# Three pieces of the mixers' elementwise work change engine: two to ScalarE, one to GpSimd

## The chip, the cores and the metric

The kernel runs on one core of a Trainium2 chip. The metric is the device time of one execution in microseconds. The core's engines are TensorE (PE: matmuls and, overlapping with them, weight loads, PEld), VectorE (DVE), ScalarE (ACT), GpSimd (POOL) and SyncE (SP, which here issues most of the DMAs). Each engine runs its own list of instructions in order; an instruction that waits holds up all that stand behind it on the same engine.

## What is computed (the reference, cut)

One decoder layer on 1024 tokens and 16 meta tokens, float32, model width 1024: half-step SwiGLU, then two mixers on the same normalised input, merged by gates, then another SwiGLU and a norm. The mixers are what matters here: a chunked gated DeltaNet (8 heads of 128) and an RWKV-7 time mixing (16 heads of 64).

```python
u = _rmsnorm(h, mix_norm[l])
aq, ak, av, az, abeta, aalpha, bcols, ga, gb = jnp.split(u @ w_in[l], ...)
o_a = _deltanet_branch(...)      # A
o_b = _rwkv7_branch(...)         # B
merged = sigmoid(ga) * o_a + sigmoid(gb) * o_b
h = h + merged @ w_out[l]

# A, per head and chunk of tokens
tinv = triangular_solve(m + eye, eye, lower=True, unit_diagonal=True)
k_tail = k * jnp.exp(g_last[..., None] - g)[..., None]
v_new = u_i - w_i @ state
o = qg_i @ state + attn_i @ v_new
state = state * exp(gl_i) + kt_i.T @ v_new

# B, the decay
w_log = -softplus(-(w0 + jnp.tanh(wd) @ w_up)) - 0.5
decay = exp(-exp(w_log))
a = sigmoid(a0 + ad @ a_up)
```

`k_tail`, the inverses and the two up-projections `w_up` and `a_up` are the three places that the change touches.

## The kernel before

The kernel has three stages: the first feed-forward block, the mixers (`middle`, about 700 to 2290 us of the profile) and the second feed-forward block. Tensors lie with channels on the 128 partitions and tokens along the free dimension. Every dense product is made of three float32r products: an operand is split into a high part (rounded, by ScalarE, L163) and a low part (the rest, by VectorE's subtraction, L164), and `mm3` (L315) multiplies high by high, high by low and low by high; the result is called `pp`, the split weights `w`, the raw ones `wraw`.

The mixers work on two segments of tokens: segment 0 has the 16 meta tokens and 512 others (528 columns, taken as 256 and 272), segment 1 has 512. For each segment there are eight iterations, one for a pair of B's heads and one of A's, so 16 in all. An iteration is made of actions that a table (`schedule`, L171) interleaves, so that three iterations are under way at once: `merge_blocks` and `transitions` of one, `operands` and `inverses` of the next, `chains`, `gates` and `finish` of the first again, then `decay`, `new_b` and `new_a` of the one after the next. From the program in this order a static scheduler makes each engine's list, by its own estimates of when operands are ready. So one edit can move instructions on all engines; nothing is reordered at run time.

The actions that matter:

- `decay` loads the raw up-projections (`upr`), makes their high parts `upz` on ScalarE (L1361) and the low parts by two 64x128 subtractions on VectorE (L1363). The products `pw` and `pa` (L1368 to L1373) use them.
- `new_b` makes B's `vB`, `kB`, `rB`, the normalised key `kkn`, the operands `AR` and `BK`, and at its end `bv` (L1438). ScalarE splits `bv` (`hl`, L163) and TensorE sums its columns (`bon`, L1289, one product with the high part and one with the low part).
- `new_a` makes A's `kq` after a short convolution (`acc`, L1466, with the carry `xr` from GpSimd) and transposes `Va` (L1478, L1479).
- `operands` (L1600 and on) transposes A's keys in four 128x128 pieces into PSUM (`ktp`), and multiplies them by `kts`, one number per partition and piece, into `ktl`. `chains` uses `ktl` one iteration later in `p3` (L1830), the update of the state. `ktl` has two buffers.
- `inverses` solves the triangular systems of all blocks by substitution on VectorE (`tb`, `Xb`, L1657 and L1659, 31 steps of two instructions), then makes a transposed copy `Yt` of the solution `Xb` (L1660). Both go by way of DRAM into `Xc` and `Y`.
- `merge_blocks` joins the blocks on TensorE (`iv`, L1692; `T` is its copy, L1713), and `transitions` uses the result (`xp`, `vp` with the copies `xa`, `at`, `xv`, L1753 to L1759).
- `chains` runs four chunks one after the other. Each has `p` (L1815), a difference on VectorE (`rhA`), `p` (L1821), a copy with a scale on ScalarE (`vn`, L1825), then `pq` (L1827, L1828) and `p` (L1830).
- `gates` makes `zg`, `gs` and `gg` by three activations each (L1211 to L1213).

Of the kernel before, what the change touches and what calls it, by code (L numbers as in the profile page):

```python
# [29 lines left out]
NCA = FULL // CA  # L30
# [1020 lines left out]
def middle(g):  # L1051
    tc, nc = g.tc, g.nc
    g.mmctx.close()
    with ExitStack() as ctx:
# [70 lines left out]
def tmp_tile(g, name, w=528):  # L1125
    return g.st.tile([P, w], F32, name=name, tag="tmp", bufs=NTMP)


def ch3(ap, c):
    return ap.rearrange("p (a b) -> p a b", b=c)  # L1130
# [151 lines left out]
def halves(n, first=256):  # L1282
    return [(0, first), (first, n - first)] if n > 512 else [(0, n)]
# [63 lines left out]
def decay(g, it):  # L1347

    nc, st, V = g.nc, g.st, g.V
    c = g.seg  # L1350
    q = K()
    q.c, q.it, q.j, q.s, q.n, q.off = c, it, it % NJ, c.s, c.n, c.off
    j, n, off = q.j, c.n, c.off
    meta = q.s == 0
    fs = slice(off, off + FULL)
    tmp = lambda name, w=528: tmp_tile(g, name, w)

    raw = st.tile([P, 2, P], F32, name="upr", tag="upr")
    nc.sync.dma_start(raw, g.a["upwa"][j])
    up = g.upz  # L1360
    nc.scalar.activation(up[:, 0:2, :], raw, AF.Copy)  # L1361
    for i, sl in enumerate(HS):
        nc.vector.tensor_tensor(up[sl, 2 + i, :], raw[sl, i, :], up[sl, i, :].bitcast(F32), op=ALU.subtract)  # L1363
    Ls, sw, av = tmp("Ls"), tmp("sw"), tmp("av")
    for c0, cn in halves(n):
        pw = g.mx.tile([P, 512], F32, name="pw", tag="mx")
        cs = slice(c0, c0 + cn)
        nc.tensor.matmul(pw[:, :cn], lhsT=up[:, 0, :], rhs=c.ws[:, cs], start=True, stop=False)  # L1368
        nc.tensor.matmul(pw[:, :cn], lhsT=up[:, 2, :], rhs=c.ws[:, cs], start=False, stop=True)
        nc.scalar.activation(sw[:, c0 : c0 + cn], pw[:, :cn], AF.Exp, scale=-1.0, bias=V("w0", j))  # L1370
        pa = g.mx.tile([P, 512], F32, name="pa", tag="mx")
        nc.tensor.matmul(pa[:, :cn], lhsT=up[:, 1, :], rhs=c.as_[:, cs], start=True, stop=False)
        nc.tensor.matmul(pa[:, :cn], lhsT=up[:, 3, :], rhs=c.as_[:, cs], start=False, stop=True)  # L1373
        nc.scalar.activation(av[:, c0 : c0 + cn], pa[:, :cn], AF.Exp, scale=-1.0, bias=V("a0", j))
    for x in (sw, av):
        nc.scalar.activation(x[:, :n], x[:, :n], AF.Ln, bias=1.0)
        nc.scalar.activation(x[:, :n], x[:, :n], AF.Exp, scale=-1.0)
    nc.vector.tensor_tensor_scan(Ls[:, :n], g.C("rsB")[:, 16 - off : 16 - off + n], sw[:, :n], 0.0,
                                 op0=ALU.mult, op1=ALU.add)
    EN = sw  # L1380
    nc.scalar.activation(EN[:, :n], Ls[:, :n], AF.Exp, scale=CDEC)
    ELx = tmp("ELx", 520).rearrange("p (c t) -> p c t", t=CB + 1)
    nc.gpsimd.memset(ELx[:, :, 0:1], 1.0)
    nc.scalar.activation(ELx[:, :, 1:], ch3(Ls[:, fs], CB), AF.Exp, scale=-CDEC)
    gam = q.gam = st.tile([P, NCB], F32, name="gam", tag="gam", bufs=2)
    nc.gpsimd.tensor_copy(gam.unsqueeze(2), ELx[:, :, CB : CB + 1])
    if meta:
        elm = q.elm = st.tile([P, 17], F32, name="elm", tag="elm", bufs=2)
        nc.gpsimd.memset(elm[:, 0:1], 1.0)
        nc.scalar.activation(elm[:, 1:17], Ls[:, 0:16], AF.Exp, scale=-CDEC)  # L1390
    q.EN, q.ELx, q.av = EN, ELx, av
    return q
# [94 lines left out]
def operands(g, q):  # L1487

    nc, st, V, c, j, n, off = g.nc, g.st, g.V, q.c, q.j, q.n, q.off
# [9 lines left out]
    for c4 in range(0, NCB, 4):  # L1499
        ps = [g.mx.tile([P, 512], F32, name="grb", tag="mx") for _ in range(2)]  # L1500
# [8 lines left out]
    if meta:  # L1509
        nc.vector.tensor_copy(g.bkpm[0:64, 0, :], g.bkm[0:64, :])  # L1510
        nc.vector.tensor_copy(g.bkpm[64:128, 1, :], g.bkm[64:128, :])
        ps = g.mx.tile([P, 512], F32, name="gbm", tag="mx")
        for h in range(2):
# [3 lines left out]
                                op=ALU.mult)  # L1517
# [3 lines left out]
    kts = st.tile([P, NCA], F32, name="kts", tag="kts")  # L1521
# [16 lines left out]
    for b in range(2):  # L1538
        ps = g.mx.tile([P, 512], F32, name="gra", tag="mx")
        for c2 in range(2):  # L1540
            i = 2 * b + c2
# [28 lines left out]
    ps = [g.mx.tile([P, 512], F32, name="bkt", tag="mx") for _ in range(2)]  # L1570
# [21 lines left out]
    if meta:  # L1592
        btm = q.btm = st.tile([64, P], F32, name="btm", tag="btm", bufs=2)
        ps = g.mx.tile([P, 512], F32, name="btp", tag="mx")
        nc.tensor.matmul(ps[:64, 0:P], lhsT=g.bkm, rhs=g.C("ident"), start=True, stop=True)
        nc.scalar.activation(btm, ps[:64, 0:P], AF.Copy)
    ktl = q.ktl = st.tile([P, NCA, P], F32, name="ktl", tag="ktl", bufs=2)
    ps = g.mx.tile([P, 512], F32, name="ktp", tag="mx")
    for i in range(NCA):
        nc.tensor.transpose(ps[:, i * P : (i + 1) * P], kq[:, 0, off + i * CA : off + (i + 1) * CA], g.C("ident"))  # L1600
    nc.vector.tensor_tensor(ktl, ch3(ps, P), kts.unsqueeze(2).to_broadcast([P, NCA, P]), op=ALU.mult)
    if meta:
        vkm = q.vkm
        ps = g.mx.tile([P, 512], F32, name="vmp", tag="mx")
# [33 lines left out]
def inverses(g, q):  # L1638

    nc, st = g.nc, g.st  # L1640
    meta = q.s == 0
    U = g.Ub
    npt = 115
    nblk = NBLK + 3 * meta
    scX = g.dram.tile([NBLK, 32, 2, 16], F32, name="scX", tag="scX", bufs=2)
    scY = g.dram.tile([NBLK + 3, 16, 2, 32], F32, name="scY", tag="scY", bufs=2)
    X = st.tile([115, 32, 16], F32, name="Xb", tag="Xb")
    Yt = st.tile([115, 16, 32], F32, name="Yt", tag="Yt")
    tmb = st.tile([115, 144], F32, name="tb", tag="tb")
    nc.gpsimd.memset(X, 0.0)  # L1650
    Xf = X.rearrange("p t c -> p (t c)")
    nc.gpsimd.memset(Xf[0:64, 0 : 33 * 15 + 1 : 33], 1.0)
    nc.gpsimd.memset(Xf[64:115, 16 : 16 + 33 * 15 + 1 : 33], 1.0)
    for i in range(31):
        nt, ncc = 31 - i, i // 2 + 1
        tv = tmb[:, : nt * ncc].rearrange("p (t c) -> p t c", c=ncc)
        nc.vector.tensor_tensor(tv, U[:, i, i + 1 :].unsqueeze(2).to_broadcast([npt, nt, ncc]),  # L1657
                                X[:, i, 0:ncc].unsqueeze(1).to_broadcast([npt, nt, ncc]), op=ALU.mult)
        nc.vector.tensor_tensor(X[:, i + 1 :, 0:ncc], X[:, i + 1 :, 0:ncc], tv, op=ALU.add)  # L1659
    nc.vector.tensor_copy(Yt, X.rearrange("p t c -> p c t"))  # L1660
    for r in range(2):
        nc.sync.dma_start(scX[:, :, r, :], X[64 * r : 64 * r + NBLK])
    for r in range(2):
        nc.sync.dma_start(scY[:nblk, :, r, :], Yt[64 * r : 64 * r + nblk])
    Y, XA = g.Y[q.it % 2], g.XA
    Xc = q.Xc = st.tile([P, 12, 2, 16], F32, name="Xc", tag="Xb")
    nc.sync.dma_start(Xc.rearrange("p t r c -> p t (r c)"), scX.rearrange("(t b) i r c -> (b i) t (r c)", b=4))
    yv = scY[:NBLK].rearrange("(t b) c r i -> b (c r) t i", b=4)
    for b in (1, 3, 0, 2):
        sl = slice(32 * b, 32 * b + 32)  # L1670
        nc.sync.dma_start(Y[sl, :, 32 * b : 32 * b + 32], yv[b])
        if b < 2:
            nc.gpsimd.tensor_copy(XA[sl, :, b, :, :], Xc[sl, NCB:])
    if meta:
        ym = q.ym = st.tile([48, 3, 16], F32, name="ym", tag="ym", bufs=2)
        ymv = scY[NBLK:, 0:8].rearrange("t c r i -> (c r) t i")
        nc.sync.dma_start(ym[32:48, 0:2], ymv[:, 0:2, 0:16])
        nc.sync.dma_start(ym[0:16, 2], ymv[:, 2, 0:16])
# [205 lines left out]
def finish(g, q):  # L1884
# [110 lines left out]
```

## Time and profile before

| | |
|---|---|
| median of 3 runs | 2974.12 us (2969.96 to 2985.99) |
| the profiled execution | 2974.08 us |
| its span, first to last instruction | 2972.3 us |
| mean granted TensorE clock | 0.993 |

How to read the views: "busy" is the time in which an engine had an instruction running. A row of the timeline has the start in us from the span's start, the duration, engine, line, operation, out<-in, the shape of the output and the input, a count of merged neighbours and, in square brackets, how long the engine was idle before it and what ended that. A row of the waits has the waiting line, what released it, the sum in us, how often, and the longest. Durations on one engine overlap a little, so the distance from one start to the next is shorter than the duration. A tile's row has the shortest, median and longest duration in ns and the first and last start.

### The profile page before, as it was taken

How to read it: one execution, taken by the hardware profiler on the slowest of the kernel's cores; microseconds unless marked ns; L12 is line 12 of the kernel's file. 1: busy time of each engine (PE TensorE's matmuls, PEld its weight loads, DVE VectorE, ACT ScalarE, POOL GpSimd, SP SyncE). 2: the span in 40 equal slices, each digit the busy share in tenths (PEclk: the TensorE clock that was granted, in tenths of full speed). 3: DMA queues.
4: the chain of work that ended last, by engine and by line, in shares of the span. 5: the costliest groups of instructions: out<-in, count | busy, mean ns of one | idle time of the engine just before them, and what ended most of it. 6: DMA issues, size and time to landing. Idle time of an engine off the chain costs nothing.

```text
span 2972.3 us, 63124 instructions
## 1 busy us (share of the span) xinstructions
PE 2876.8 (97%) x25720; PEld 2496.4 (84%) x25720; DVE 2208.8 (74%) x4121; ACT 1450.5 (49%) x2559; POOL 503.4 (17%) x578
## 2 busy tenths in 40 slices
PE   8999999999899999999998999999999999999998
PEld 8999999999878888888776777777777888888887
DVE  8666668776667877788878887778876766667886
ACT  6322234346555656565566556556644422223443
POOL 0332232323000000000000000001101032332431
PEclk9999999999999999999999999999999999999999
DMA  5333236553232322333232332333345332333763
GB/s 212 125 108 108 98 124 206 182 193 118 71 70 72 86 65 68 84 81 85 89 98 73 80 79 77 76 87 82 106 132 185 127 109 99 97 102 130 248 220 113
DMA packets 287907, 339.39 MB, mean 114 GB/s; under 512 B 172704, under 2 KB 181024, under 8 KB 287616
## 3 DMA queue, kind: packets, MB, share of 16 engines
q1 hardware_dynamic: 283600, 326.17, 36.0%
q0 software_dynamic: 2000, 6.56, 0.6%
q8 instruction: 202, 3.31, 0.5%
q10 hardware_dynamic: 2016, 2.63, 0.2%
q14 instruction: 89, 0.73, 0.1%
HBM read 267.63 MB, written 73.41 MB: 115 GB/s over the span
## 4 chain that ended last, share of the span: by engine, by line
PE 67%; DVE 19%; ACT 6%; issue 3%; DMA 3%; SPq 1%; POOL 0%; DVEq 0%; ACTq 0%; POOLq 0%
PE pg L521 25%; PE pp L315 15%; PE pd L742 10%; DVE w L164 3%; PE pwo L315 2%; PE pg L545 2%; DVE tb L1657 1%; DVE Xb L1659 1%; DVE form L164 1%; ACT w L163 1%; PE vp L1342 1%; DMA form<-frm 1%; PE mp L1342 1%; PE xp L1342 1%; PE np L1342 1%
## 5 line engine op out<-in xcount | busy, mean ns | idle before, releaser
L315 PE MATMUL pp<-uk,w 128*128 128x512 f32 (+2 forms) x4824 | 971.3, 347 | 13.8 <-DVE w L164 5.9
L315 PEld LDWEIGHTS pp<-uk,w 128*128 128x128 f32 x4824 | 745.4, 191 | 111.7 <-DVE w L164 14.7
L742 PE MATMUL pd<-form,w 128*128 128x256 f32 (+2 forms) x2904 | 437.3, 312 | 5.4 <-DVE w L164 5.2
L742 PEld LDWEIGHTS pd<-form,w 128*128 128x128 f32 x2904 | 402.7, 189 | 39.5 <-DVE w L164 7.3
L521 PE MATMUL pg<-bt,w 128*128 128x256 f32 (+2 forms) x2520 | 401.9, 318 | 3.1 <-DVE w L164 2.5
L521 PEld LDWEIGHTS pg<-bt,w 128*128 128x128 f32 x2520 | 360.2, 188 | 37.3 <-DVE w L164 3.8
L527 DVE TENSOR_TENSOR c<-c,pg 128x520 f32<-128x520 f32 (+1 forms) x280 | 189.4, 688 | 239.1 <-PE pg L521 215.8
L164 DVE TENSOR_TENSOR w<-wraw,w 128x1024 fp32r<-128x1024 f32 (+1 forms) x254 | 338.2, 1332 | 38.7 <-ACT w L163 37.1
L521 PE MATMUL pg<-b,w 128*128 128x256 f32 (+2 forms) x2160 | 348.1, 317 | 0.0
L163 ACT ACTIVATE w<-wraw 128x1024 fp32r<-128x1024 f32 (+1 forms) x254 | 266.9, 1052 | 164.1 <-PE pg L521 117.4
L521 PEld LDWEIGHTS pg<-b,w 128*128 128x128 f32 x2160 | 309.9, 188 | 28.3 <-DVE w L164 0.3
L163 ACT ACTIVATE w<-wrx 128x1024 fp32r<-128x1024 f32 (+1 forms) x64 | 58.4, 912 | 279.0 <-PE pg L521 239.2
L491 POOL TENSOR_TENSOR wrx<-wrx 128x512 f32<-128x512 f32 x38 | 52.5, 1381 | 612.8 <-DVE w22b L164 351.6
L164 DVE TENSOR_TENSOR form<-form 128x520 fp32r<-128x520 f32 (+1 forms) x152 | 145.8, 995 | 14.0 <-ACT form L163 13.8
L163 ACT ACTIVATE w<-wsum 128x768 fp32r<-128x768 f32 x96 | 75.6, 788 | 155.8 <-PE pd L742 117.1
L164 DVE TENSOR_TENSOR w<-wsum,w 128x768 fp32r<-128x768 f32 x96 | 112.9, 1181 | 37.3 <-ACT w L163 37.3
L163 ACT ACTIVATE form<-form 128x520 fp32r<-128x520 f32 (+1 forms) x152 | 93.8, 631 | 79.5 <-DMA form<-frm 73.4
L242 POOL TENSOR_TENSOR wsum<-wsum,wraw 128x768 f32<-128x768 f32 (+1 forms) x48 | 97.6, 2050 | 204.7 <-DMA wraw<-in_wdn 154.3
L1659 DVE TENSOR_TENSOR Xb<-Xb,tb 115x126 f32<-115x126 f32 (+22 forms) x496 | 125.2, 252 | 8.7
L1657 DVE TENSOR_TENSOR tb<-Ub,Xb 115x126 f32<-115x126 f32 (+22 forms) x496 | 124.5, 251 | 9.5 <-DMA Ub<-scr 2.0
L1466 DVE SCALAR_TENSOR_TENSOR acc<-xr,pk,acc 128x528 f32<-128x528 f32 (+1 forms) x144 | 109.0, 757 | 20.6 <-ACT acc L1462 19.9
L315 PE MATMUL pwo<-uk,w 128*128 128x512 f32 x384 | 95.3, 397 | 1.3 <-DVE uk L164 0.6
(439 smaller groups left out, 4421.4 us busy)
## 6 DMA issues: line engine op xcount, KB each, us to landing
wraw<-in_win SPq DMA_DIRECT2D x150, 512.0 KB
wraw<-in_wgu SPq DMA_DIRECT2D x44, 512.0 KB
wrx<-in_wgu SPq DMA_DIRECT2D x44, 512.0 KB
frm<-c SPq DMA_DIRECT2D x76, 260.0 KB
form<-frm SPq DMA_DIRECT2D x76, 260.0 KB
frm<-c SPq DMA_DIRECT2D x76, 256.0 KB
form<-frm SPq DMA_DIRECT2D x76, 256.0 KB
wraw<-in_wdn SPq DMA_DIRECT2D x34, 384.0 KB
```

Of the source, the lines that this page charges most:

```text
L163: g.nc.scalar.activation(hi, src, AF.Copy)
L164: (eng or g.nc.vector).tensor_tensor(lo, src, hi.bitcast(F32), op=ALU.subtract)
L242: g.nc.gpsimd.tensor_tensor(s, x, y, op=ALU.add if r == 1 else ALU.subtract)
L315: g.last_product = g.nc.tensor.matmul(ps, lhsT=l, rhs=r, start=i == 0, stop=i == n - 1)
L521: nc.tensor.matmul(ps[:, c0 : c0 + cn], lhsT=l[:, x, k, :], rhs=r[:, k, y, c0 : c0 + cn], start=i == 0, stop=i == 3 * HK - 1)
L527: nc.vector.tensor_tensor(o, x, y, op=ALU.add)
L545: nc.tensor.matmul(ps[:, c0 : c0 + cn], lhsT=l[:, x, k, :], rhs=r[:, k, y, c0 : c0 + cn], start=i == 0, stop=i == 6 * HK - 1)
L742: nc.tensor.matmul(pd[:, c0 : c0 + cn], lhsT=wd[:, u, k - k0, :], rhs=x[:, v, c0 : c0 + cn], start=k + i == 0, stop=k == HF - 1 and i == 2)
L1342: g.nc.tensor.matmul(ps[e][HS[dst], c0 : c0 + CB], lhsT=l, rhs=r, start=True, stop=True)
L1466: nc.vector.scalar_tensor_tensor(acc[:, :n], xr[:, tap : tap + n], V("convw", ct * 4 + tap), acc[:, :n], op0=ALU.mult, op1=ALU.add)
L1657: nc.vector.tensor_tensor(tv, U[:, i, i + 1 :].unsqueeze(2).to_broadcast([npt, nt, ncc]), X[:, i, 0:ncc].unsqueeze(1).to_broadcast([npt, n ...
L1659: nc.vector.tensor_tensor(X[:, i + 1 :, 0:ncc], X[:, i + 1 :, 0:ncc], tv, op=ALU.add)
```

## The change

Three edits, each made once in every one of the 16 iterations:

- the two subtractions that make the low parts of `upz` go from VectorE to GpSimd;
- `ktl`, one VectorE multiplication of 128x512 out of PSUM, becomes four ScalarE activations of 128x128 with a scale per partition;
- `Yt`, the transposed copy, goes from VectorE to ScalarE.

```diff
@@ decay
     for i, sl in enumerate(HS):
-        nc.vector.tensor_tensor(up[sl, 2 + i, :], raw[sl, i, :], up[sl, i, :].bitcast(F32), op=ALU.subtract)
+        nc.gpsimd.tensor_tensor(up[sl, 2 + i, :], raw[sl, i, :], up[sl, i, :].bitcast(F32), op=ALU.subtract)
@@ operands
-    nc.vector.tensor_tensor(ktl, ch3(ps, P), kts.unsqueeze(2).to_broadcast([P, NCA, P]), op=ALU.mult)
+    for i in range(NCA):
+        nc.scalar.activation(ktl[:, i], ps[:, i * P : (i + 1) * P], AF.Identity, scale=kts[:, i : i + 1])
@@ inverses
-    nc.vector.tensor_copy(Yt, X.rearrange("p t c -> p c t"))
+    nc.scalar.activation(Yt, X.rearrange("p t c -> p c t"), AF.Copy)
```

Lines behind L1601 have a number higher by one after the change. The scheduler puts other instructions of the mixers in another order too. Three places, all in an iteration of segment 1:

VectorE at the end of the solve, before (the rows run from `rB` to the step ahead of `bv`, all of `new_b` but `Yt`, `w` and `upz`; `t` is a work tile):

```order
L1203 SCALAR_TENSOR_TENSOR rB<-pp,pk,rB 128x512
L1660 COPY Yt<-Xb 115x512
L1436 TENSOR_TENSOR AR<-rB,ELx 128x8x64
L164 TENSOR_TENSOR w<-wraw,w 128x1024
L1419 SCALAR_TENSOR_TENSOR kkn<-kB,pk,kkn 128x512
L1363 TENSOR_TENSOR upz<-upr,upz 64x128
L1421 TENSOR_TENSOR t_23650<-av,kkn 128x512
L1429 TENSOR_TENSOR AR<-kkn,ELx 128x8x64
L1426 SCALAR_TENSOR_TENSOR BK<-t_23650,sw 128x8x64
L1423 TENSOR_TENSOR kB<-kB,av 128x512
L1363 TENSOR_TENSOR upz<-upr,upz 64x128
L1425 TENSOR_TENSOR BK<-kB,sw 128x8x64
```

and after:

```order
L1203 SCALAR_TENSOR_TENSOR rB<-pp,pk,rB 128x512
L1436 TENSOR_TENSOR AR<-rB,ELx 128x8x64
L1419 SCALAR_TENSOR_TENSOR kkn<-kB,pk,kkn 128x512
L1421 TENSOR_TENSOR t_22616<-av,kkn 128x512
L1429 TENSOR_TENSOR AR<-kkn,ELx 128x8x64
L1426 SCALAR_TENSOR_TENSOR BK<-t_22616,sw 128x8x64
L1423 TENSOR_TENSOR kB<-kB,av 128x512
L164 TENSOR_TENSOR w<-wraw,w 128x1024
L1425 TENSOR_TENSOR BK<-kB,sw 128x8x64
L1438 SCALAR_TENSOR_TENSOR bv<-rB,pk,kB 128x512
```

`Yt` and both `upz` are gone, and one low part of the weights, `w`, has moved from ahead of `kkn` to behind `kB`. Ahead of `bv` stand three instructions fewer.

TensorE, first around `bon`, then around the transposes `ktp` of `operands` and the first chunk of `chains`. Before:

```order
L1289 MATMUL cs<-hl,bdr 128x512 x2
L315 MATMUL pp<-uk,w 128x512 x38
L1289 MATMUL bon<-hl,bdr 128x512
...
L1600 MATMUL ktp<-ck,kq 128x128 x4
L1821 MATMUL p_23250<-rhA,Y_7681 128x128
L1840 MATMUL b_23252<-SBs,mt 128x64
L315 MATMUL pp<-uk,w 128x512 x3
L1827 MATMUL pq<-kq,SA 128x128
L1828 MATMUL pq<-attn,vn 128x128
L315 MATMUL pp<-uk,w 128x512 x2
L1830 MATMUL p_23260<-vn,ktl 128x128
```

and after:

```order
L1289 MATMUL cs<-hl,bdr 128x512 x2
L315 MATMUL pp<-uk,w 128x512 x35
L1289 MATMUL bon<-hl,bdr 128x512
...
L1600 MATMUL ktp<-ck,kq 128x128 x4
L1822 MATMUL p_23289<-rhA,Y_7681 128x128
L1841 MATMUL b_23291<-SBs,mt 128x64
L315 MATMUL pp<-uk,w 128x512 x6
L1828 MATMUL pq<-kq,SA 128x128
L1829 MATMUL pq<-attn,vn 128x128
L1831 MATMUL p_23299<-vn,ktl 128x128
```

`bon` stands three projection matmuls earlier. At the chunk three more stand ahead of `pq`, and the two between `pq` and the state's update are gone from there. On ScalarE the four `ktl` activations stand directly ahead of this chunk's `vn`.

ScalarE between `operands`' decays and the copies of `transitions`, before (`kts` are the numbers that scale `ktl`):

```order
L1533 ACTIVATE kts<-kts 128x4
L1211 ACTIVATE zg<-pp 128x512
L1479 ACTIVATE Va<-vap 128x512
L1713 ACTIVATE T_22814<-iv_22813 64x256
L1212 ACTIVATE zg<-zg 128x512
L163 ACTIVATE w<-wraw 128x1024
L1213 ACTIVATE zg<-zg 128x512
L1755 ACTIVATE xa<-xp 128x4x64 x2
```

and after:

```order
L1533 ACTIVATE kts<-kts 128x4
L1211 ACTIVATE zg<-pp 128x512
L163 ACTIVATE w<-wraw 128x1024
L1479 ACTIVATE Va<-vap 128x512
L1714 ACTIVATE T_22850<-iv_22849 64x256
L1212 ACTIVATE zg<-zg 128x512
L1213 ACTIVATE zg<-zg 128x512
L1756 ACTIVATE xa<-xp 128x4x64 x2
```

The high part of a weight, `w`, has moved from behind `T` to ahead of `Va` and `T`; the same instructions stand ahead of `xa`.

## The prediction

> **What bounds the kernel now.** The page's first line gives the busy time of each engine and its share of the span.
>
> ```profile
> PE 2876.8 (97%) x25720; PEld 2496.4 (84%) x25720; DVE 2208.8 (74%) x4121; ACT 1450.5 (49%) x2559; POOL 503.4 (17%) x578
> ```
>
> TensorE is busy 97% of the span. Whatever the other engines do can give back at most the remaining 2972.3 - 2876.8 = 95.5 us, and only where TensorE waits for them. The change is confined to the mixers, about 700 to 2290 us, so the next view is TensorE's waits in that stretch (microseconds in total, times, longest):
>
> ```profile
> PE bon L1289 <- ACT hl L163: 12.3, 14, 1.5
> PE pp L315 <- DVE w L164: 5.9, 7, 2.8
> ...
> PE vp L1342 <- ACT xv L1757: 5.1, 15, 0.4
> ...
> PE pp L315 <- ACT acc L1462: 3.0, 1, 3.0
> PE vap L1478 <- DVE acc L1470: 2.4, 6, 0.4
> ...
> PE iv L1692 <- DMA Xc<-scX: 1.7, 1, 1.7
> ```
>
> These six rows hold 30.4 us, a third of those 95.5. The largest ends on ScalarE's split of `bv` (`hl`), which itself waits for VectorE; `vp` waits for a plain ScalarE copy out of PSUM. Then one stage by itself, an iteration of each segment (columns: window, its length, busy time of PE, PEld, DVE, ACT and POOL with counts, granted clock, DMA share, GB/s):
>
> ```profile
> 1146.00:1240.00 94.00, 91.42 (x1127) 78.69 (x1126) 72.67 (x182) 56.27 (x115) 6.42 (x22) 1.00 0.30 76
> 1814.00:1901.00 87.00, 83.88 (x941) 66.86 (x942) 70.53 (x167) 52.83 (x101) 8.10 (x15) 1.00 0.30 82
> ```
>
> The granted clock is 1.00 in both. TensorE has 2.6 and 3.1 us free per iteration; VectorE has 21.3 and 16.5 us free, ScalarE 37.7 and 34.2. So VectorE isn't short of time over an iteration. It can only be late at particular places, and the work that the change removes counts only if it stands just ahead of one.
>
> **What the change takes off VectorE, and what of it lies on the path.**
>
> ```profile
> L1660 DVE COPY Yt<-Xb x16: 597/609/619, 839.0 to 2212.8; 115x512 f32<-115x512 f32 x16
> L1601 DVE TENSOR_TENSOR ktl<-ktp,kts x16: 691/691/692, 794.5 to 2168.5; 128x512 f32<-128x512 f32 x16
>   PE ktp L1600: 31.7, 16
> L1363 DVE TENSOR_TENSOR upz<-upr,upz x32: 274/288/292, 713.9 to 2039.2; 64x128 fp32r<-64x128 f32 x32
> ```
>
> VectorE loses 16 x (0.609 + 0.691 + 2 x 0.288) = 30.0 us of its 2208.8. That is no gain yet. The scaled transposes `ktl` come out of idle time: the third row says that VectorE sat idle 31.7 us in front of them, about 2 us each time, until TensorE had delivered `ktp`. What VectorE does next (the scaling of `kq`, L1607) is wanted only an iteration later. I count `ktl` at **0**.
>
> The other two stand close together at the end of the triangular solve, in segment 1 just ahead of the end of `new_b`. VectorE there (start, duration):
>
> ```profile
> 1859.34 0.61 DVE L1660 COPY Yt<-Xb 115x512 f32<-115x512 f32 x1
> 1859.87 0.68 DVE L1436 TENSOR_TENSOR AR<-rB,ELx 128x512 f32<-128x512 f32 x1
> ...
> 1862.27 0.29 DVE L1363 TENSOR_TENSOR upz<-upr,upz 64x128 fp32r<-64x128 f32 x1
> 1862.47 0.69 DVE L1421 TENSOR_TENSOR t<-av,kkn 128x512 f32<-128x512 f32 x1
> ...
> 1864.28 0.69 DVE L1423 TENSOR_TENSOR kB<-kB,av 128x512 f32<-128x512 f32 x1
> 1864.99 0.29 DVE L1363 TENSOR_TENSOR upz<-upr,upz 64x128 fp32r<-64x128 f32 x1
> 1865.32 0.69 DVE L1425 TENSOR_TENSOR BK<-kB,sw 128x512 f32<-128x512 f32 x1
> 1865.93 0.75 DVE L1438 SCALAR_TENSOR_TENSOR bv<-rB,pk,kB 128x512 f32<-128x512 f32 x1
> ```
>
> No row shows an idle time, so `bv` moves forward by what is taken out ahead of it. By start-to-start steps: `Yt` 0.53, the first low part 0.20, and around the second the step from `kB` to `BK` shrinks from 1.04 to the 0.60 of its neighbours, 0.44. Together **1.17 us**. ScalarE and TensorE then follow:
>
> ```profile
> 1866.71 0.63 ACT L163 ACTIVATE hl<-bv 128x512 fp32r<-128x512 f32 x1 [0.69 <-DVE bv L1438]
> 1867.39 0.50 PE L1289 MATMUL bon<-hl,bdr 128*128 128x512 f32 x1 [1.52 <-ACT hl L163]
> 1869.59 6.31 PE L315 MATMUL pp<-uk,w 128*128 128x512 f32 x27
> ```
>
> TensorE waits 1.52 us here. But the changed order also calls `bon` 3 projection matmuls earlier (35 ahead of it instead of 38), and one of those takes 6.31 / 27 = 0.23 us by the last row, so the wait starts 0.68 us earlier. What is left of the gain is 1.17 - 0.68 = 0.49 us. Of the 14 waits in the `bon` row above, five are of this kind, 1.3 to 1.5 us, all in segment 1 behind the turn between the segments: **-2.5 us**.
>
> In segment 0 the same place reads differently:
>
> ```profile
> 1202.13 0.60 DVE L1660 COPY Yt<-Xb 115x512 f32<-115x512 f32 x1
> 1202.65 0.68 DVE L1426 SCALAR_TENSOR_TENSOR BK<-t,sw 128x512 f32<-128x512 f32 x1
> ...
> 1204.81 1.51 PE L315 MATMUL pp<-uk,w 128*128 128x272 f32 x11
> 1206.82 0.50 PE L1289 MATMUL bon<-hl,bdr 128*128 128x512 f32 x1 [0.50 <-ACT hl L163]
> PE pp L315 <- DVE w L164: 0.2, 1, 0.2
> ```
>
> The low parts ran 20 us earlier there, so only `Yt`, 0.52 us, stands ahead of `bv`; `bon` is called three 272-column matmuls earlier, 0.41 us (11 of them take 1.51). That leaves 0.11 us of a 0.50 us wait, and I add most of the 0.2 us by which TensorE waits for a `w` low part in this iteration (the last row, from its waits), 0.3 together, since those parts queue on VectorE behind the removed work. Five iterations: **-1.5 us**. The first inversion is the only one for which TensorE waits on the way through DRAM (`iv`, 1.7 us once); ScalarE can take that copy as soon as the solve is done, without the VectorE work that now runs in between, which I estimate at one 0.5 us step: **-0.5 us**.
>
> **What it adds to ScalarE.** `Yt` there has no row. The nearest are the same copy on VectorE, 0.61, and a 128x512 activation, `hl`, 0.63; I take 0.6. A `ktl` piece is 128x128 with a scale per partition:
>
> ```profile
> 1820.85 0.40 ACT L1825 ACTIVATE vn<-p,tk 128x128 f32<-128x128 f32 x1
> 1848.58 0.29 ACT L163 ACTIVATE ug<-ugr 128x128 fp32r<-128x128 f32 x1
> 1821.63 0.39 PE L1828 MATMUL pq<-attn,vn 128*128 128x128 f32 x2
> ```
>
> `vn` has that very form, 0.40 alone; a plain copy of this size takes 0.29. Four cost 1.16 to 1.6, and since neighbours on ScalarE overlap I take 1.15. Altogether 16 x (0.6 + 1.15) = 28 us, in an engine with 34 us free per iteration. The question is again only where.
>
> The four pieces stand right in front of `vn` of the first chunk, whose product TensorE needs next. The new order answers with three more projection matmuls ahead of that product, 0.68 us, and moves the two that stood behind it: cover of 0.68 against 1.15, on top of the 0.4 us that lay between `vn`'s end (1821.25) and its use (1821.63). About 0, at the long end 1.6 - 1.08 = 0.5 us in each of 16 iterations, so **0, bounds 0 and +8 us**. `Yt` goes between the two steps of `kkn` in segment 1; the 0.69 us of idle time ahead of `hl` is the cover for its 0.6, and if that is gone it takes back half of the 1.17.
>
> What the diff doesn't say, but the order does: in segment 1 a weight split `w` now goes ahead of `Va` and `T`.
>
> ```profile
> 1889.20 0.38 ACT L1713 ACTIVATE T<-iv 64x256 f32<-64x256 f32 x1
> ...
> 1890.14 1.04 ACT L163 ACTIVATE w<-wraw 128x1024 fp32r<-128x1024 f32 x1
> ```
>
> `T` starts the products that join the inverse's blocks, and `xa` waits for those. It comes later by `w`'s 1.04 us; the number of instructions in front of `xa` stays as it was. Bounds 0 and 1.04 in five iterations (5.2 us); other projections fill some of it and I take 0.4: **+2.0 us**.
>
> **What it adds to GpSimd.** The rows near a 64x128 subtraction are a 128x512 one from the weights' stage, and tiny copies beside a fully occupied VectorE:
>
> ```profile
> L491 POOL TENSOR_TENSOR wrx<-wrx 128x512 f32<-128x512 f32 x38 | 52.5, 1381 | 612.8 <-DVE w22b L164 351.6
> 1847.21 2.30 POOL L1386 COPY gam<-ELx 128x8 f32<-128x8 f32 x1 [10.68 <-ACT ELx L1384]
> 1888.13 0.19 POOL L1535 COPY egl<-gp 128x4 f32<-128x4 f32 x1 [10.26 <-ACT kts L1533]
> 1846.93 0.75 DVE L1897 SCALAR_TENSOR_TENSOR yb<-yb,pk,bv 128x512 f32<-128x512 f32 x1
> L1368 PEld LDWEIGHTS pw<-ws,upz x24: 186/188/193, 719.2 to 2099.0; 128*128 128x128 f32 x24
> ```
>
> A quarter of the columns gives 1.38 / 4 = 0.35 us; a copy of 8 columns took 2.30. So 0.35 to 2.3 each. Nobody waits: between the last low part (2039.2) and the last product that loads it (2099.0) lie 60 us, and in the first iteration (713.9 and 719.2) 5.3 us, which hold even two long ones. Behind it on GpSimd stand the carries of the convolution and `gam`, with an idle time of 10.68 us ahead of it. Counted at **0** for itself.
>
> The same rows show who pays when the two engines meet: `gam` is stretched to 2.30 against 0.19 for `egl`, while the VectorE operation that runs beside it, on two SBUF operands, keeps the 0.75 of its kind (`bv`). The Trainium skill, "SBUF — State Buffer", section "SBUF: two separate sides", says that a VectorE operation with two SBUF inputs and a GpSimd operation that reads SBUF share a port pair under an exclusive lock: whichever starts first holds it for its whole instruction and the other blocks. By that rule, which speaks against the change, VectorE is blocked whenever GpSimd gets in first, and the sum would be higher by the 3.5 to 11 us of the third rival; no row here shows VectorE paying, and by the rows the sum stays as it is.
>
> **The sum**, against the profiled execution's own 2974.08 us (span 2972.3 and 1.8 around it, practically the median of 2974.12): -2.5 - 1.5 - 0.5 + 2.0 = -2.5, so **2971.6 us**. The turn between the segments (1600 to 1727) has single stalls of 3.0 and 2.8 us, the last column of two rows above; the new order rearranges it, and I take 0 with bounds of -5.8 and +5.8.
>
> **Rivals.**
> - *The relief passes in full.* TensorE's order soaks up nothing and VectorE's part of the waits goes: 12.3 + 5.9 + 2.4 = 20.6 us, giving **2953.5**. For it: these rows all end on VectorE or just behind it. Against it: `bon` is called earlier, and `ktl` came out of idle time. Chance 0.13.
> - *ScalarE's queue becomes what TensorE waits for*, slower. ScalarE works in order, and `xv` and `hl` already end waits with no slack. If one misplaced `w` (1.04) lands in a chain in each of 15 iterations, +15.6: **2989.7**; if all of `ktl` and `Yt` does (1.75), about **3000**. It decides once an addition exceeds the filler that the order puts beside it: 1.15 against 1.08 at `vn` is already close. Against it: 34 us free per iteration. Chance 0.13.
> - *GpSimd blocks VectorE.* Two low parts of 0.35 us in five iterations of segment 1, beside the stretch that ends in `bv`: +3.5 us; in all 16, +11. That eats the forecast's gain: **2974.5 to 2982**. Chance 0.20.
> - *It does nothing*, everything being hidden: **2974**. Chance 0.12.
>
> **How the numbers follow.** The forecast, -2.5 us, has the remaining 0.42; by the bounds of its terms it runs from 2966 (the turn's -5.8) to 2983 (`vn` at +8, `T` at +5.2 in place of +2.0). The range reaches down to the first rival's 2953 and up to 2986 (the 2983 with the port's +3.5); it leaves out the slow rival and little else. About 0.5% of the time, 15 us, is what a measurement of this kernel can tell from no change. Faster than 2959: 0.13; slower than 2989: 0.13; within: 0.74.
>
> **What would show each step.** In the changed profile the `bon` wait in segment 1 should read 0.9 to 1.1 instead of 1.5, and 0.3 to 0.4 in segment 0; VectorE's busy time should fall by 30 us and ScalarE's rise by 28. If the second rival is right, waits for `vn`, `T` or `xa` appear or `xp` and `vp` grow by more than 0.5 us per iteration. If GpSimd blocks, VectorE's rows beside `upz` are longer than their 0.69 and 0.75. The forecast is wrong if the time moves while these waits stand still, for the place would then be one that I did not look at, above all the turn between the segments.

## The result, and the profile after

The changed kernel is slower: 2988.62 us median of 8 runs (2980.16 to 3001.09) against 2974.14 of 8 runs before (2969.96 to 2985.99), a ratio of 1.0051 with a 95% interval of 1.0037 to 1.0065. The forecast was 2971.6, its range ended at 2986.

The profiled execution after the change took 2980.16 us, the fastest of its eight. So two things have to be found: the 6.1 us by which its span is longer (2978.4 against 2972.3), and why the other executions are slower still. First the busy times, then TensorE's waits in the mixers (columns as before):

```profile
PE 2875.2 (97%) x25720; PEld 2499.4 (84%) x25720; DVE 2188.7 (73%) x4057; ACT 1480.6 (50%) x2639; POOL 523.3 (18%) x610
```

```profile
PE pp L315 <- DVE w L164: 16.3, 13, 2.4
PE bon L1289 <- ACT hl L163: 7.5, 9, 2.0
PE np L1342 <- DVE AR L1769: 7.2, 15, 1.0
PE vp L1342 <- ACT xv L1758: 5.6, 15, 0.4
PE xp L1342 <- ACT at L1754: 4.6, 13, 0.6
PE vap L1478 <- DVE acc L1470: 3.1, 8, 1.1
PE iv L1717 <- ACT T L1714: 2.9, 7, 0.6
```

The `bon` row has shrunk from 12.3 to 7.5 us, but the row above it, the low part of the weights `w`, has grown from 5.9 to 16.3. Where that is, the distances between the `ktp` transposes of successive iterations tell. Up to the tenth of them the changed kernel is 5.7 us ahead. From there to the sixteenth it loses 10.1 us: the five steady iterations of segment 1 take 88.3 to 89.8 us instead of 86.9 to 87.4, which is 8.8 of those 10.1. Their TensorE, in the one that starts at 1906 us:

```profile
1944.72 6.08 PE L315 MATMUL pp<-uk,w 128*128 128x512 f32 x26
1953.12 2.37 PE L315 MATMUL pp<-uk,w 128*128 128x512 f32 x9 [2.32 <-DVE w L164]
1955.32 0.39 PE L1289 MATMUL bon<-hl,bdr 128*128 128x512 f32 x1
```

After 26 products TensorE stands for 2.32 us until the low part of the next weights is there. `bon`, nine products on, waits no more. One step further up is ScalarE:

```profile
1945.04 0.68 ACT L1308 ACTIVATE kkn<-cs,pk 128x512 f32<-128x512 f32 x1
1946.42 1.12 ACT L1661 ACTIVATE Yt<-Xb 115x512 f32<-115x512 f32 x1 [0.70 <-DVE Xb L1660]
1947.45 0.61 ACT L1310 ACTIVATE kkn<-kkn 128x512 f32<-128x512 f32 x1
1947.98 1.04 ACT L163 ACTIVATE w<-wraw 128x1024 fp32r<-128x1024 f32 x1
```

`Yt` stands ahead of `kkn` and `w`. It waits 0.70 us for the last step of the solve on VectorE, with ScalarE idle and both others ready behind it, and then takes 1.12 us. Before the change `w` started 0.57 us after `kkn<-cs`; now it is 2.94 us. The place in an iteration before the change, ScalarE and then VectorE:

```profile
1857.40 0.68 ACT L1308 ACTIVATE kkn<-cs,pk 128x512 f32<-128x512 f32 x1
1857.97 1.06 ACT L163 ACTIVATE w<-wraw 128x1024 fp32r<-128x1024 f32 x1
1858.91 0.63 ACT L1310 ACTIVATE kkn<-kkn 128x512 f32<-128x512 f32 x1
...
1860.47 1.22 DVE L164 TENSOR_TENSOR w<-wraw,w 128x1024 fp32r<-128x1024 f32 x1
1861.61 0.75 DVE L1419 SCALAR_TENSOR_TENSOR kkn<-kB,pk,kkn 128x512 f32<-128x512 f32 x1
```

VectorE's part of the same stretch after the change:

```profile
1948.10 0.75 DVE L1419 SCALAR_TENSOR_TENSOR kkn<-kB,pk,kkn 128x512 f32<-128x512 f32 x1 [0.33 <-ACT kkn L1310]
1948.89 0.69 DVE L1421 TENSOR_TENSOR t<-av,kkn 128x512 f32<-128x512 f32 x1
1949.50 0.95 DVE L1429 TENSOR_TENSOR AR<-kkn,ELx 128x512 f32<-128x512 f32 x1
1950.37 0.95 DVE L1426 SCALAR_TENSOR_TENSOR BK<-t,sw 128x512 f32<-128x512 f32 x1
1951.25 0.68 DVE L1423 TENSOR_TENSOR kB<-kB,av 128x512 f32<-128x512 f32 x1
1951.85 1.21 DVE L164 TENSOR_TENSOR w<-wraw,w 128x1024 fp32r<-128x1024 f32 x1
...
1953.59 0.77 DVE L1438 SCALAR_TENSOR_TENSOR bv<-rB,pk,kB 128x512 f32<-128x512 f32 x1
```

In the new order the low part stands behind `kB`. It ends at 1953.06, and TensorE goes on at 1953.12. Two further things show here: VectorE has to wait for `kkn` (0.33), and two of its rows take 0.95 us instead of 0.69. So `bv` isn't earlier at all: from ScalarE's `kkn<-cs` to `bv` it is 8.55 us, before the change 8.53 (1865.93 in the prediction's rows less 1857.40). And `w` is late first of all by its place on VectorE: ScalarE's part of it was done at 1949.02, but five other operations, from `kkn` at 1948.10 on, stand ahead of the low part. The two long rows run beside GpSimd's `upz`:

```profile
1949.40 1.37 POOL L1363 TENSOR_TENSOR upz<-upr,upz 64x128 fp32r<-64x128 f32 x2 [12.25 <-ACT upz L1361]
```

The other part is the clock. The mean granted clock of the eight runs after the change is 0.990, of 76 runs of the kernel before 0.9924. On 2975 us 0.0025 of the clock is 7.4 us, about half of the 14.5. In the profiled execution one of the five `w` waits is followed by a drop. The window that holds it and the one of the next wait:

```profile
1770.00:1780.00 10.00, 7.99 (x29) 6.14 (x28) 8.51 (x11) 3.88 (x7) 3.92 (x7) 0.83 0.74 160
1860.00:1870.00 10.00, 7.70 (x34) 6.03 (x33) 9.76 (x13) 3.96 (x7) 4.62 (x7) 1.00 0.78 173
```

A clock of 0.83 over 10 us is 1.7 us lost, behind a wait of 2.02 us; the wait of 2.30 us in the second window passed without. Whether the drops belong to the waits is taken up under the experiments.

### The profile page after: what moved, and what is told of

Its sections match the earlier page's. It is cut to its first block, busy times and chain, and to the rows that moved or that the text cites. A ratio compares the mean times of both kernels' runs of the same rounds, so it can differ in the third digit from the quotient of the medians.

```text
span 2978.4 us, 63187 instructions
## 1 busy us (share of the span) xinstructions
PE 2875.2 (97%) x25720; PEld 2499.4 (84%) x25720; DVE 2188.7 (73%) x4057; ACT 1480.6 (50%) x2639; POOL 523.3 (18%) x610
## 4 chain that ended last, share of the span: by engine, by line
PE 67%; DVE 18%; ACT 8%; issue 4%; DMA 3%; SPq 1%; POOL 0%; DVEq 0%; ACTq 0%; POOLq 0%
PE pg L521 24%; PE pp L315 15%; PE pd L742 10%; DVE w L164 3%; PE pwo L315 2%; DVE tb L1658 2%; DVE Xb L1660 2%; PE pg L545 1%; ACT w L163 1%; DVE form L164 1%; PE xp L1342 1%; PE vp L1342 1%; DMA form<-frm 1%; PE mp L1342 1%; DVE mt L1766 1%
## 5 line engine op out<-in xcount | busy, mean ns | idle before, releaser
L315 PE MATMUL pp<-uk,w 128*128 128x512 f32 (+2 forms) x4824 | 973.9, 348 | 21.8 <-DVE w L164 16.3
```

Source lines behind the costliest of these rows:

```text
L315: g.last_product = g.nc.tensor.matmul(ps, lhsT=l, rhs=r, start=i == 0, stop=i == n - 1)
```

## The experiments

Four theories, named as in the expectations. A: `Yt` at the head of ScalarE's queue. B: the scheduler's new place of `w` on VectorE. C: GpSimd holds VectorE up. D: `ktl` delays `vn`. The ratios are against runs of the kernel before on the same chip; the last column is the mean granted clock of the timed runs.

| kernel | median us | ratio, 95% interval | clock |
|---|---|---|---|
| the change | 2988.6 | 1.0051 [1.0037, 1.0065] | 0.990 |
| only `Yt` | 2989.9 | 1.0048 [1.0031, 1.0065] | 0.990 |
| only `ktl` | 2978.8 | 1.0020 [1.0005, 1.0034] | 0.992 |
| only `upz` | 2982.7 | 1.0020 [1.0007, 1.0033] | 0.991 |
| `ktl` and `upz` | 2974.0 | 0.9997 [0.9986, 1.0009] | 0.993 |
| the change, `Yt` queued behind `kkn` | 2973.1 | 0.9994 [0.9984, 1.0005] | 0.992 |
| the change, `Yt` read in order | 2990.1 | 1.0052 [1.0036, 1.0068] | 0.990 |
| `ktl`, `Yt` behind `kkn`, `upz` on VectorE | 2981.7 | 1.0023 [1.0012, 1.0035] | 0.991 |
| the change, low products last | 2966.2 | 0.9972 [0.9959, 0.9984] | 0.990 (0.993 but for one run that reads 0.966) |
| before, `bv` later | 3004.7 | 1.0097 [1.0077, 1.0117] | 0.987 |
| before, low products last | 2964.5 | 0.9968 [0.9955, 0.9981] | 0.994 |
| `Yt` behind `kkn` and low products last | 2962.8 | 0.9955 [0.9940, 0.9970] | 0.993 |

**The parts one by one.** First only the copy:

```diff
-    nc.vector.tensor_copy(Yt, X.rearrange("p t c -> p c t"))
+    nc.scalar.activation(Yt, X.rearrange("p t c -> p c t"), AF.Copy)
```

> Only Yt goes to ScalarE; ktl and upz stay on VectorE. Here VectorE keeps the low part w ahead of kkn, as before the change; only ScalarE has Yt ahead of kkn and w. Theory A (Yt stands at the head of ScalarE's queue, waits there for the end of the solve, and makes kkn and w late, about 2 us per iteration of segment 1): +5 to +14 us, a TensorE wait of 1.5 to 2.5 us in each of five iterations, ending on bon or w. Theory B (it needs VectorE's new place of w, behind kB): within 3 us of before. Theory C (GpSimd blocks VectorE) and theory D (ktl delays vn): within 3 us of before.

Its loss is as large as that of the whole change, 2989.9 (14.3 us, just above the upper end that A gave). TensorE's waits in segment 1 (1640 to 2260 us):

```profile
PE pp L315 <- DVE w L164: 7.9, 10, 1.8
PE pp L315 <- ACT w L163: 5.5, 4, 2.0
```

But it doesn't separate A from B. In three of the five iterations `Yt` waits ahead of `kkn` and `w` on ScalarE, and there, against the expectation, VectorE has the low part behind `kB`, as in the change:

```profile
1953.97 1.11 ACT L1660 ACTIVATE Yt<-Xb 115x512 f32<-115x512 f32 x1 [0.71 <-DVE Xb L1659]
...
1958.24 0.68 DVE L1423 TENSOR_TENSOR kB<-kB,av 128x512 f32<-128x512 f32 x1
1958.84 1.22 DVE L164 TENSOR_TENSOR w<-wraw,w 128x1024 fp32r<-128x1024 f32 x1
...
1960.11 2.34 PE L315 MATMUL pp<-uk,w 128*128 128x512 f32 x9 [1.77 <-DVE w L164]
```

These three have waits of 1.47, 1.77 and 1.77 us, without a drop of the clock. In the change the same iterations wait 2.02, 2.32 and 1.77; the first two have GpSimd's `upz` in this stretch, the last has not, so about 0.55 us of the wait is GpSimd's part. In the other two iterations `Yt` doesn't wait and VectorE has the low part ahead of `kkn`; they lose most, 10.8 of the 13.6 us that the five lose in the profiled execution. That is the second row, a form that no theory had foreseen: about 11 us ahead of `Yt` the high part of another `w` comes too late, twice in short succession (1.97 and 0.79 us in one of them), and the clock drops. So the size of the loss is that of the change, the make of it only in part.

```diff
-    nc.vector.tensor_tensor(ktl, ch3(ps, P), kts.unsqueeze(2).to_broadcast([P, NCA, P]), op=ALU.mult)
+    for i in range(NCA):
+        nc.scalar.activation(ktl[:, i], ps[:, i * P : (i + 1) * P], AF.Identity, scale=kts[:, i : i + 1])
```

> Only ktl goes to ScalarE. Theory D (the four activations ahead of vn delay each first chunk of chains): +5 to +10 us, with waits of pq for vn in the trace. Theories A, B and C: within 3 us of before.

It is 0.2% slower, and D has no part in it: no wait of `pq` for `vn` shows. The distances of the iterations agree with those of before within 1.2 us in the steady part but for one, the first behind the turn between the segments, which takes 92.6 us instead of 86.9. There the order has the late `w` of ScalarE again (a wait of 1.94 us), and the clock drops behind it (0.50 for 6.8 us, 3.4 us lost).

```diff
-        nc.vector.tensor_tensor(up[sl, 2 + i, :], raw[sl, i, :], up[sl, i, :].bitcast(F32), op=ALU.subtract)
+        nc.gpsimd.tensor_tensor(up[sl, 2 + i, :], raw[sl, i, :], up[sl, i, :].bitcast(F32), op=ALU.subtract)
```

> Only the low parts of upz go to GpSimd. Theory C (GpSimd holds VectorE up; after the change two VectorE instructions beside upz took 0.95 us instead of 0.69): the same two long rows here, and if they lie on the path up to +0.5 us in each of 16 iterations, +3 to +8 us. Theories A, B, D: -3 to +1 us, since 0.58 us per iteration leave VectorE, ahead of bv in segment 1.

Also 0.2% slower, with the long rows that C expects. VectorE beside the two subtractions:

```profile
1774.95 1.47 DVE L164 TENSOR_TENSOR w<-wraw,w 128x1024 fp32r<-128x1024 f32 x1
1776.35 0.95 DVE L1419 SCALAR_TENSOR_TENSOR kkn<-kB,pk,kkn 128x512 f32<-128x512 f32 x1
1777.34 0.69 DVE L1421 TENSOR_TENSOR t<-av,kkn 128x512 f32<-128x512 f32 x1
```

`w` takes 1.47 instead of 1.22 us, `kkn` 0.95 instead of 0.75. So VectorE pays 0.45 us for the 0.64 (0.20 and 0.44 by steps) that it was relieved of; from ScalarE's `kkn<-cs` to `bv` it takes 8.58 us as against 8.53 before. The order had counted on the relief and calls `bon` one product, 0.23 us, earlier:

```profile
1781.94 0.50 PE L1289 MATMUL bon<-hl,bdr 128*128 128x512 f32 x1 [1.79 <-ACT hl L163]
1782.28 3.03 PE L315 MATMUL pp<-uk,w 128*128 128x512 f32 x7
```

The wait grows from 1.5 to 1.8 us, and the seven products behind it take 3.03 us instead of 1.75. That is the clock: the profile has a drop behind four of the five waits of 1.8 to 1.9 us, and a single `bon` wait of 6.6 us at the turn between the segments besides.

The whole change but for `Yt` (the `ktl` and `upz` edits together):

> The whole change but for Yt, which stays on VectorE. Theory A and theory B: the loss is gone, 2968 to 2976 us, and the spread of the runs is that of before (nearly all within 3 us), with the pp<-w waits of segment 1 gone. Theory C: +3 to +8 us. Theory D: +5 to +10 us.

2974.0 us, a ratio of 0.9997: A and B hold, and C and D by themselves are refuted as causes of the loss. The two edits cost 0.2% each alone and nothing together, so what they cost alone is, by the rows above, a matter of the order that the scheduler makes for each program.

**The place of `Yt`.** Here `Yt` and what follows it are emitted after `kkn` of the iteration behind its own, and queued behind it on ScalarE:

```diff
+def solution(g, q, behind=None):
+    ...
+        if behind:
+            after.enter_context(g.tc.issue_after(behind.ins))
+        nc.scalar.activation(Yt, X.rearrange("p t c -> p c t"), AF.Copy)
...
-        nc.scalar.activation(out[:, :n], out[:, :n], AF.Exp, scale=-0.5)
+        g.last_exp = nc.scalar.activation(out[:, :n], out[:, :n], AF.Exp, scale=-0.5)
...
+    if it and g.unsolved:
+        solution(g, g.unsolved.pop(), g.last_exp)
```

> The whole change, with Yt still on ScalarE but queued behind kkn (its copy and what follows it are emitted later in the program); w goes ahead of kkn again on ScalarE and VectorE. Theory A (the loss is Yt's place: it waits at the head of ScalarE's queue for the end of the solve): the pp<-w waits of about 2 us in segment 1 are gone, 2966 to 2977 us, clock 0.992 or more. Rival A2 (Yt costs on ScalarE wherever it stands, 1.12 us of work): 2982 us or more, with av, hl and bon late.

2973.1 us: the loss is gone though `Yt` takes as long as in the change. ScalarE now:

```profile
1857.02 1.06 ACT L163 ACTIVATE w<-wraw 128x1024 fp32r<-128x1024 f32 x1
1857.97 0.63 ACT L1316 ACTIVATE kkn<-kkn 128x512 f32<-128x512 f32 x1
1858.49 1.13 ACT L1679 ACTIVATE Yt<-Xb 115x512 f32<-115x512 f32 x1
1859.51 0.41 ACT L1367 ACTIVATE upz<-upr 128x256 fp32r<-128x256 f32 x1
1861.59 0.82 ACT L1430 ACTIVATE av<-av,pk 128x512 f32<-128x512 f32 x1 [1.66 <-DVE t L1429]
```

`Yt` lies in time that ScalarE then spends waiting for `t` anyway. This decides for A against A2. It leaves B open, for on VectorE too `w` stands ahead of `kkn` again: in no steady iteration of segment 1, of any run, does `Yt` wait ahead of `w` on ScalarE while VectorE keeps `w` ahead of `kkn`, nor the reverse. The `pp<-w` waits of segment 1 are gone and `bon`'s are back, 6.1 us in 1640 to 2260, the longest 1.3.

The copy in the other direction of reading:

```diff
-    nc.scalar.activation(Yt, X.rearrange("p t c -> p c t"), AF.Copy)
+    nc.scalar.activation(Yt.rearrange("p c t -> p t c"), X, AF.Copy)
```

> The whole change, with Yt's copy reading Xb in its own order and writing transposed, the same values. Theory E (Yt takes 1.12 us on ScalarE, not 0.6, because it reads 16 elements apart): 0.6 to 0.7 us, the w wait in segment 1 shorter by 0.5 us, some 4 to 6 us faster than the change. If it still takes 1.1 us, the reading order isn't the reason. By theory A most of the loss stays either way: 2980 to 2988 us.

E is refuted: 1.18 us (median of 16), and the loss is that of the change. A copy in order, added to the kernel with `Yt` behind `kkn`, separates the rest:

```diff
+        nc.scalar.activation(tmp_tile(g, "plain")[0:115, 0:512], X.rearrange("p t c -> p (t c)"), AF.Copy)
```

> The change with Yt behind kkn, and a second ScalarE copy of the same 115x512 in order, into an unused tile, behind it: extra work, the result is not changed. Only its row is wanted. Theory E2 (the transposition costs the time on ScalarE): 0.60 to 0.65 us against Yt's 1.12. If it takes 1.1 too, the 115 partitions or the tile are the reason.

```profile
L1680 ACT ACTIVATE plain<-Xb x16: 614/622/641, 823.8 to 2201.1; 115x512 f32<-115x512 f32 x16
```

0.62 us against 1.12: on ScalarE the transposition costs the time, on whichever side it stands; VectorE made the same transposed copy in 0.61.

With `Yt` behind `kkn`, but the low parts back on VectorE:

> As the run with Yt queued behind kkn, but the low parts of upz back on VectorE, so that nothing is added to GpSimd. Theory C2 (what GpSimd takes from VectorE it gives back as lengthened VectorE instructions, about 0.26 us each, two per iteration): within 3 us of the run with upz on GpSimd, and w, kkn, AR and BK at their 1.21, 0.75, 0.68 us. If the move to GpSimd is a gain in itself: 2 to 5 us slower than it.

This missed: it is 8.6 us slower than with GpSimd. But `w` and `kkn` are at their old lengths (means of 1.22 and 0.75 us), and its five `bon` waits are at most 0.8 us. What it has is the late `w` of ScalarE at 1763 us, 1.97 us and a drop to 0.72 over 12 us, and a mean clock of 0.991. So GpSimd's effect by itself can't be read from this pair; the order hides it.

**The low part.** If the loss comes in by way of the low part, it should be cured by wanting that part later:

```diff
-    for k in range(kk):
-        hi, lo = rhs(k)
-        for l, r in ((w[:, 0, k, :], hi), (w[:, 0, k, :], lo), (w[:, 1, k, :], hi)):
-            ... matmul(ps, lhsT=l, rhs=r, ...)
+    for lw in range(2):
+        for k in range(kk):
+            for r in rhs(k)[: 2 - lw]:
+                ... matmul(ps, lhsT=w[:, lw, k, :], rhs=r, ...)
```

> The whole change as it is, but each dense product does all 16 products with the weights' high part first and the 8 with the low part last (same products, other order of the sum), so that the low part w may be 14 matmuls, 3.2 us, later. Theory A: the loss comes in by way of the late low part, so the pp<-w waits of 1.8 to 2.4 us in segment 1 vanish; 2966 to 2976 us and clock 0.992 or more, unless the late high part (rows pp<-ACT w) or bon takes their place. A rival by which the loss sits elsewhere (ktl, GpSimd): within 4 us of the change, 2984 to 2992.

It is: 2966.2 us, 22 less than the change and 0.28% faster than before. In four of the five steady iterations `Yt` still waits ahead of `kkn` and `w` on ScalarE, and `w` still stands behind `kB` on VectorE; in 1640 to 2260 no `pp` wait is left in the list, and `bon` has 7.7 us. The same order without the change, and with `Yt` behind `kkn`:

> Before the change, with the weights' low-part products last. If the gain of 22 us that this order gave on top of the change is all the loss being hidden plus before's own w waits (5.9 us), this runs at 2964 to 2970 us, equal to the changed kernel with the same order. If the change itself brings something once its loss is hidden, this is 3 to 8 us slower than that one: 2969 to 2974.

> The change with Yt queued behind kkn and the low-part products last, both together. If both cure the same wait, no more than with the low-part products last alone: 2962 to 2970 us. If the late kkn, bv and bon behind Yt cost something of their own, 3 to 6 us faster than that: 2958 to 2963.

2964.5 and 2962.8 us. Some 10 of the 22 us are thus what this order gives the kernel before as well; the other 12 are most of the loss of 14.5. With the wait for the low part gone the change brings nothing that can be measured (0.9972 against 0.9968), and the third kernel, the fastest of all at 0.9955, can't be told from the second by these intervals.

**The clock.** Is a drop the consequence of a longer wait?

```diff
     nc.vector.scalar_tensor_tensor(bv, r[:, fs], V("rk", j), k[:, fs], op0=ALU.mult, op1=ALU.mult)
+    if not meta:
+        nc.vector.scalar_tensor_tensor(bv, bv, 1.0, bv, op0=ALU.mult, op1=ALU.max)
```

> Before the change, with a second VectorE operation on bv in segment 1 (bv * 1.0, maximum with itself: the same values), so that bon's wait in segment 1 grows from 1.5 to about 2.1 us (bv comes some 1.5 us later, and the new order calls bon four matmuls, 0.9 us, later). Theory G (waits of about 2 us and more trip the granted clock at times, and each trip costs another 1.7 us): median 2981 to 2987 us, mean clock 0.990 to 0.991, with drops right behind bon in segment 1. Rival (the clock has nothing to do with these waits): only the wait itself, +0.6 us in five or six iterations, 2976 to 2980 us, mean clock 0.992 to 0.993 as before.

3004.7 us, more than either expected, and not as planned: the new order turned the wait for `bon` into waits for ScalarE's `w`, in the same form as above, in all five iterations.

```profile
1851.17 0.73 PE L315 MATMUL pp<-uk,w 128*128 128x512 f32 x2 [1.96 <-ACT w L163]
1852.70 0.80 PE L315 MATMUL pp<-uk,w 128*128 128x512 f32 x1 [0.79 <-ACT w L163]
```

```profile
1850.00:1860.00 10.00, 7.55 (x19) 5.25 (x20) 9.59 (x28) 3.04 (x6) 0.42 (x1) 0.66 0.45 144
```

Behind all five the clock drops, here by 3.4 us' worth in a window. Over the profiles of the twelve kernels of the table and of before, single TensorE waits of more than 1.2 us between 1640 and 2260 us fall into two groups:

| single wait | how many | followed by a drop |
|---|---|---|
| 1.27 to 1.54 us | 20 | 0 |
| 1.71 to 2.32 us | 29 | 15 |
| of these: 1.94 to 1.97 us for ScalarE's `w`, with 0.4 to 0.8 us more close behind | 9 | 9 |

Before the change all six such waits lie at 1.32 to 1.52 us, and none has a drop. Which of the longer waits drop is settled by where they lie. In each profile the clock changes only at the ends of equal steps of 3.41 us. The first two rows are the step with the change's wait of 2.02 us and the one behind it, the other two the steps into which its wait of 2.30 us falls:

```profile
1771.03:1774.44 3.41, 1.40 (x7) 0.85 (x5) 3.41 (x5) 2.52 (x4) 1.85 (x3) 1.00 0.68 107
1774.45:1777.86 3.41, 3.41 (x10) 2.67 (x9) 3.41 (x6) 0.63 (x1) 1.51 (x3) 0.50 0.80 206
1859.78:1863.19 3.41, 1.93 (x9) 1.27 (x7) 3.40 (x5) 2.98 (x6) 2.42 (x4) 1.00 0.66 85
1863.20:1866.60 3.40, 2.59 (x11) 2.16 (x12) 3.40 (x5) 1.02 (x2) 1.62 (x3) 1.00 0.75 182
```

The first wait leaves TensorE idle for 2.01 us of one step, and the next step has half the clock; the second is cut into 1.48 and 0.82, and nothing follows. So it is with all of them: in these thirteen profiles and this stretch the 15 drops from full clock follow steps with 1.79 to 2.68 us idle, and no other step at full clock has more than 1.76. So here a wait costs 1.7 to 3.4 us more than its length once about 1.8 us of it fall into one step. Outside this stretch drops also follow steps with less idle time, so this is no rule for other code. The experiment was meant to change nothing but one wait and changed the order too; a wait lengthened by itself was not tried.

## Why the prediction was wrong, point by point

**The failed step** is "`bv` moves forward by what is taken out ahead of it", 1.17 us by the sum, with its cover on ScalarE: "`Yt` goes between the two steps of `kkn` in segment 1; the 0.69 us of idle time ahead of `hl` is the cover for its 0.6". In the rows above `bv` has moved by nothing (8.55 us behind `kkn<-cs`, 8.53 before). `Yt` takes 1.12 us, not 0.6, and waits 0.70 for the solve with `kkn` and `w` behind it; so VectorE waits 0.33 us for `kkn`. By start-to-start steps the two rows beside GpSimd's `upz` take back 0.54 more, and three steps that are longer by about 0.1 each take the rest. With nothing gained, three products fewer ahead of `bon` (0.68 us) only lengthen TensorE's wait, from 1.5 to 2.3. It falls on `w` and not on `bon` because that `w` had moved on VectorE from ahead of `kkn` to behind `kB`; the move stood in the order that the prediction was made from, and no term of the sum has it. By the runs the wait is 1.8 to 2.3 us where `bon` had 1.3 to 1.5, and the clock adds its part: 14.5 us in all. Shown is that the loss comes with `Yt` on ScalarE ahead of `kkn` and `w` (it is gone with `Yt` on VectorE or behind `kkn`) and by way of the low part (it is gone when that is wanted later). How much is `Yt`'s own wait and how much the new place of `w` that comes with it stays open.

**The second rival** (ScalarE's queue becomes what TensorE waits for, 2989.7) named the engine and the reason, work in order, and came within 1.1 us, at a chance of 0.13. Its price was right by accident: not 1.04 us in 15 iterations, but some 1.2 to 2.9 us in five, and the rest by the clock. Of its signs only the waits for `T` came, which the sum had itself; those for `vn` and `xa` did not. The order's sign that should have raised its chance was `Yt` ahead of `kkn` and `w` while its own input came from the end of VectorE's longest chain. The rivals at 2953.5 and 2974 are refuted by the time.

**The gain at `bon`** (-2.5 in segment 1): the wait is gone altogether, where 0.9 to 1.1 was predicted, but only because TensorE had waited for `w` nine products ahead. With `Yt` queued behind `kkn` the wait is back at what was predicted, 1.00 to 1.05 us in four iterations and 0.62 in the last. That is luck in part: there `bv` comes 0.70 us earlier instead of 1.17, and one product is missing ahead of `bon` instead of three (0.23 instead of 0.68), so that 0.47 is left where the sum had 0.49.

**Segment 0 and the first inversion** (-1.5 and -0.5): between the first and the eighth `ktp` the changed kernel gains 2.0 us, as the sum has it, but not as the sum spreads it: 2.6 in the first of these iterations, a loss of 2.0 in the next two, 1.4 over the last four. The wait for `Xc` at the first inversion fell from 1.7 to 1.0 us, 0.7 where 0.5 was taken. `bon` in the iteration at 1141 us waits 0.6, though, not 0.3 to 0.4. The turn between the segments, taken at 0 with bounds of 5.8, gave 3.0 us (from the ninth to the eleventh `ktp`).

**`ktl` at 0**: right for VectorE and, as to `vn`, for ScalarE. The four pieces take 1.17 us in a row of the timeline, the 1.15 that was taken, and no `pq` wait for `vn` is in the list; TensorE waits for `ktl` itself once, 1.0 us. ScalarE's busy time rose by 30.1 us (28 forecast), VectorE's fell by 20.1, not 30; if each of the 32 parts lengthened a neighbour by 0.20 to 0.26, that is 6 to 8 of the 10 missing.

**`T` at +2.0**: a row `iv` waiting for `T` has 0.4 us in each of five iterations, 2.1 us between 1640 and 2260 us, where before the change none is in the list. That term was right.

**GpSimd** (third rival): the mechanism is there, 0.20 to 0.26 us on each of two VectorE instructions per iteration, where the rows of before had shown only GpSimd paying. The Trainium skill, "SBUF — State Buffer", section "SBUF: two separate sides", had the rule, that whichever starts first holds the shared ports; the rows of the run with `upz` alone (1.47 and 0.95 us) agree with it in that VectorE pays too, though by less than the 0.45 us that GpSimd's operation takes at the least. The prediction should have given it more than the 0.20. (Its price by its own terms is 2975.1 to 2982.8, not 2974.5 to 2982.) It isn't the cause of the loss, for with `Yt` out of the way the kernel with `upz` on GpSimd runs as before; but it is 0.54 us of the 1.17 that didn't reach `bv`.

**The clock** had no place in the prediction. It read 1.00 in the windows of both stages, and the profile's mean of 0.993 was taken as fixed.

## What to carry to other kernels

An instruction that is moved to a less busy engine waits there too, and everything ready behind it waits with it: look at when its input comes and what stands behind it in the new queue, before its duration. What is taken off one engine counts only as far as nothing else in its chain comes later: check the end of the chain, not the work removed. In this kernel, bound by TensorE, it paid more to let TensorE ask later for what comes last (with the low-part products at the end it is 0.3% faster than before, with or without the change) than to shift small work between engines. Where a static scheduler makes the order, a part of a change tried alone is another program: two edits that cost 0.2% each alone cost nothing together.

## What the runs showed of the hardware

- **Waits of TensorE have a step in their price.** Of 20 waits of 1.27 to 1.54 us none, of 29 of 1.71 to 2.32 us 15 were followed by a drop of the granted clock to 0.50 for one or two steps of 3.41 us, worth 1.7 or 3.4. In 1640 to 2260 us a drop from full clock came exactly where TensorE had been idle for 1.79 us or more of one step; 1.76 us was too little. So which waits drop depends on where they lie on the steps: in the change one of five, with `upz` alone four of five. The Trainium skill, "TensorE: Matmul & The Clock Gate", section "What's actually happening", has a free-running window of 3.4 us and half the clock; the steps of 3.41 us at 0.50 agree. It gives an idle window of some 3.4 us as the condition; here 1.8 us idle in one window were enough.
- **Times mostly follow the clock from run to run.** The change's eight runs reach from 2980.2 us at 0.993 to 3001.1 at 0.985: 20.9 us for 0.008 of the clock, 0.008 of the span being 23.8. One run with the low products last read 0.966 at 2967.3 us, a time like that of the others, so a single reading can mislead.
- **A transposed copy of 115x512 costs ScalarE 1.12 to 1.18 us and a plain one 0.62**; VectorE made the transposed one in 0.61.
- **GpSimd's subtraction of 64x128** took 0.45 to 2.7 us beside VectorE (32 in the change, median 0.48), and lengthened VectorE's neighbours by 0.20 to 0.26 us.
